# A hybrid attention encoder step: the norm's row factor moved from the activations onto values, queries and keys

## The chip, the cores and the metric

One NeuronCore of a Trainium2 chip runs the whole step in one launch. The metric is the device time in microseconds (us) of that launch; lower is better. Engines are named as in the profile: PE is TensorE (matmuls; PEld are its weight loads), ACT is ScalarE, DVE is VectorE, POOL is GpSimd, and SP is the queue from which all DMA transfers of this kernel are issued.

## The reference

The program is one layer of a streaming encoder on 2048 prompt rows and 32 sample rows of width 1024, all in float32.

```
a = rmsnorm(x, g_attn)                 # x * rsqrt(mean(x*x) + eps) * g, row by row
qa, ka, va, qb, kb, vb = split(a @ w_in)       # 6 x 512 columns
oa = differential attention of qa, ka, va      # 4 heads, two maps each, chunk-causal
ob = band attention of qb, kb, vb              # 8 heads, 64-row chunks and the 8 before
h  = x + concat(norm(oa), norm(ob)) @ w_out
h  = h + relu(norm(h) @ w_up)**2 @ w_down
h  = h + sigmoid(h @ w_ple_gate) * (p @ w_ple_proj)
y  = rmsnorm(h, g_final)
```

Outputs are y and the keys and values of both groups. The sample rows attend to cached keys and values as well. What matters below is the first line: the factor r = rsqrt(mean(x*x) + eps) is one number per row, so (x * r * g) @ W is r times ((x * g) @ W).

## The kernel before, in words

Float32 products are made of three matmuls. Each operand is split into a high part that TensorE takes exactly (`hi`, type fp32r) and the rest (`lo`), and `mm3` (L187) issues hi*hi, hi*lo and lo*hi into one PSUM bank. `split` (L167) makes the parts: a cast on ACT or DVE for `hi`, a subtraction on POOL or DVE for `lo`. `wunit` (L178) loads a 512 KB piece of a weight matrix through one of two staging buffers `wr` and splits it into `wh` and `wl`.

The rows are worked in four blocks of 512 (block 3 has the 32 sample rows too). `prep` (L320) makes the normed activations of a block, 128 rows (a token tile) at a time: load x; ACT squares it and sums each row (L329); `rsqrt` (L195) makes r in three small ACT and four small DVE operations; PE transposes r, broadcast, into `rp` (L334), and ACT copies it to `rb` (L336); PE transposes x in two halves of four 128x128 pieces, each half in one PSUM bank `xp` (L342); ACT copies each half to `xt` (L343), which is stored as xT for the later residual; DVE multiplies each piece by g and rb (L346) into `a32`; DVE casts this to `aH`, POOL subtracts to get `aL`.

`proj` (L359) multiplies by w_in. The values of a group come in two columns of 256; for each column all token tiles of a half are worked (24 matmuls of 256 columns into `vps`), copied from PSUM by ACT (L384), split, and stored. Then for each of four pairs of heads come queries (`kind` 0, scaled by 0.125, L427 and L428) and keys (`kind` 1, L433), 24 matmuls of up to 512 columns each into `qps`. Results go to DRAM scratch, from which the attention loads them.

The order in `run` (L1132): blocks 0 and 1 are normed, then projected for group A (differential); then the first half of group A's attention, the band projections of blocks 0 and 1, woven with `prep` of blocks 2 and 3, band attention, and so on; later attention runs among the MLP's matmuls. In the first stage `prep` uses three PSUM banks of the pool `s`; `prep` of blocks 2 and 3 shares the two banks `mm` with the projections. The order written in the program isn't the order on the engines: a planner with its own estimates of time places every instruction on its engine's queue, from priorities that follow the program's order. Each engine then works its queue strictly in that order. The field `nt` (L139, L1266) is the number of temporary buffers of tag `tmp`, used by `raw_o` (L826) and others.

Of the kernel before, what the change touches and what calls it, by code (L numbers as in the profile page):

```python
# [133 lines left out]
class Kern:  # L134
    def __init__(self, tc, a):
        self.tc = tc
        self.nc = tc.nc
        self.a = a
        self.nt = 4  # L139
# [38 lines left out]
    def wunit(self, src, shape, hi_eng="act", lo_eng="pool"):  # L178
# [3 lines left out]
        hi = self.wp.tile([P] + shape, F32R, tag="wh", bufs=3, name="wh")  # L182
        lo = self.wp.tile([P] + shape, F32R, tag="wl", bufs=3, name="wl")
        self.split(hi, lo, raw, hi_eng, lo_eng)
        return hi, lo
# [9 lines left out]
    def rsqrt(self, pool, src, n, scale, eps, eng, tag="rs", np_=P, bufs=None):  # L195
# [9 lines left out]
        eng.tensor_tensor(y0, y0, v, op=ALU.mult)  # L205
        return y0
# [7 lines left out]
    def consts(self, cp):  # L214
# [13 lines left out]
        self.g_attn = cols("g_attn_s", a["g_attn"][0], 8)  # L228
        self.g_mlp = cols("g_mlp_s", a["g_mlp"][0], 8)
# [90 lines left out]
    def prep(self, b, acts, pp, mm, tag):  # L320
        nc = self.nc
        aH, aL = acts[b]
        for c0, n in toks(b):
# [3 lines left out]
            a32 = pp.tile([P, 8, P], F32, tag="a32", name="a32")  # L327
            st = pp.tile([P, 1], F32, tag="st", name="st")
            nc.scalar.activation(  # L329
                a32[:n].rearrange("p a b -> p (a b)"), x[:n], AF.Square, accum_out=st[:n]  # L330
            )
            r = self.rsqrt(pp, st[:n], 1, 1.0 / D, EPS, nc.vector, "r1", n)
            rp = mm.tile([P, 512], F32, tag=tag, name="rp")
            nc.tensor.transpose(rp[:, :n], r.broadcast_to([n, P]), self.ident[:n, :n])  # L334
            rb = pp.tile([P, P], F32, tag="rb", name="rb")
            nc.scalar.activation(rb[:, :n], rp[:, :n], AF.Copy)  # L336
            xt = pp.tile([P, 8, P], F32, tag="xt", name="xt")
            for h in range(2):
# [4 lines left out]
                nc.scalar.activation(xt[:, 4 * h : 4 * h + 4, :n], xp[:, :, :n], AF.Copy)  # L343
                for k in range(4):
                    kk = 4 * h + k
                    nc.vector.scalar_tensor_tensor(  # L346
                        a32[:, kk, :n], xp[:, k, :n], self.g_attn[:, kk : kk + 1], rb[:, :n],
                        op0=ALU.mult, op1=ALU.mult,
                    )
            self.dma(self.xT[:, :, t0 : t0 + n], xt[:, :, :n])  # L350
            self.split(aH[:, :, c0 : c0 + n], aL[:, :, c0 : c0 + n], a32[:, :, :n], "dve", "pool")
# [6 lines left out]

    def proj(self, half, grp, acts, sg, mm, tp, vs=range(2), gs=range(4)):  # L359
# [3 lines left out]
        nh, dv = (4, 128) if grp == 0 else (8, 64)  # L363
        hc = nh // 2
        vo_p, vo_s = (a["va_p"], a["va_s"]) if grp == 0 else (a["vb_p"], a["vb_s"])
        ko_p, ko_s = (a["ka_p"], a["ka_s"]) if grp == 0 else (a["kb_p"], a["kb_s"])
        for c in vs:
            col = base + 1024 + 256 * c
            wv = W[:, col : col + 256].rearrange("(k p) c -> p k c", p=P)
            u = [self.wunit(wv[:, 4 * i : 4 * i + 4], [4, 256]) for i in range(2)]  # L370
            for b in half:
                aH, aL = acts[b]
                for c0, n in toks(b):
                    t0 = 512 * b + c0
                    ps = mm.tile([P, 512], F32, tag="mm", name="vps")
                    self.mm3(
                        ps[:n, :256],
                        [
                            (aH[:, k, c0 : c0 + n], aL[:, k, c0 : c0 + n], u[k // 4][0][:, k % 4], u[k // 4][1][:, k % 4])
                            for k in range(8)  # L380
                        ],
                    )
                    raw = sg.tile([P, 256], F32, tag="vraw", bufs=2, name="vraw")
                    nc.scalar.activation(raw[:n], ps[:n, :256], AF.Copy)  # L384
                    hl = sg.tile([P, hc, 2, dv], F32R, tag="vhl", bufs=2, name="vhl")
                    r3 = raw.rearrange("p (h d) -> p h d", d=dv)
                    self.split(hl[:n, :, 0], hl[:n, :, 1], r3[:n], "dve", "pool")
                    row = t0 if t0 < SP else t0 + PAST
                    self.dma(
                        self.vS[grp][row : row + n, 512 * c : 512 * c + 512],  # L390
                        hl[:n].rearrange("p a b d -> p (a b d)"),
                    )
                    if t0 >= SP:
                        self.dma(vo_s[0:n, 256 * c : 256 * c + 256], raw[:n])
                    elif grp == 0:
                        self.dma(vo_p[t0 : t0 + n, 256 * c : 256 * c + 256], raw[:n])
                    elif t0 >= SP - 512:
                        self.dma(
                            vo_p[t0 - SP + 512 : t0 - SP + 512 + n, 256 * c : 256 * c + 256], raw[:n]
                        )  # L400
                    yield
# [941 lines left out]
```

## Time and profile before

| | us |
|---|---|
| median of 3 runs (lowest, highest) | 3227.9 (3224.61, 3232.49) |
| profiled execution | 3221.24 |
| its span | 3219.5 |
| PE busy | 3063.0 |
| ACT busy | 1689.7 |
| POOL busy | 1706.1 |
| DVE busy | 1552.4 |

A line of the windows gives the stretch, its length, the busy time and the number of instructions of PE, PEld, DVE, ACT and POOL, the clock granted to PE (1.00 is full), the mean busy share of the DMA engines and GB/s. A line of the groups gives the program line, the engine and operation, output and inputs with shapes, the count, busy us and mean ns, and behind the second bar the idle time before these instructions with what ended it. A line of the waits gives who waited for whom, us in total, how often, and the longest. A line of the order of time gives start and duration. The mean of a matmul (about 290 ns at 256 columns) is its latency; matmuls overlap, so their pace is read from their starts.

### The profile page before, as it was taken

What the parts mean: (1) busy time and instruction counts of PE and PEld (TensorE: products, weight loads), DVE (VectorE), ACT (ScalarE), POOL (GpSimd) and SP (SyncE); (2) the same over time, 40 slices, a digit from 0 to 9 for tenths busy, and PEclk for the clock granted to TensorE, in tenths of its full rate; (3) what the DMA queues carried; (4) which work ended last, traced back from release to release, by engine and by line L of the source; (5) the groups of instructions that cost most, each with busy time, mean ns of one, the idle gap of its engine ahead of it and who ended that gap; (6) DMA issues with size and microseconds to landing.
All of it is one profiled execution on the core that took longest, in us unless ns stands there. A gap on an engine that the chain in (4) does not pass through costs nothing.

```text
span 3219.5 us, 51107 instructions
## 1 busy us (share of the span) xinstructions
PE 3063.0 (95%) x17881; PEld 2687.7 (83%) x17881; DVE 1552.4 (48%) x3952; ACT 1689.7 (52%) x3717; POOL 1706.1 (53%) x2515
## 2 busy tenths in 40 slices
PE   6988989999998999899999999999999999999998
PEld 6877778889887888778788888878789999999988
DVE  5116776444464555576565566636532223223335
ACT  4226776666565766576566666644443322322255
POOL 5446766432345444565554555587954333333387
PEclk9999999999999999999999999999999999999999
DMA  7579876986787653654755444357431111111122
GB/s 235 164 251 264 236 226 205 264 226 182 211 248 215 190 146 105 166 161 137 215 137 143 125 135 124 119 159 252 147 114 47 47 47 47 46 46 47 60 86 88
DMA packets 503272, 487.89 MB, mean 152 GB/s; under 512 B 36924, under 2 KB 392576, under 8 KB 503016
## 3 DMA queue, kind: packets, MB, share of 16 engines
q1 hardware_dynamic: 503016, 484.64, 51.6%
q8 instruction: 141, 2.31, 0.3%
q14 instruction: 115, 0.94, 0.1%
HBM read 378.52 MB, written 109.95 MB: 152 GB/s over the span
## 4 chain that ended last, share of the span: by engine, by line
PE 54%; DMA 4%; DVE 4%; POOL 2%; ACT 2%; issue 1%; SPq 0%; DVEq 0%; POOLq 0%; ACTq 0%
PE ups L192 7%; PE dps L191 7%; PE ups L191 7%; PE ups L193 7%; PE dps L193 7%; PE dps L192 7%; PE s L585 2%; PE gps L191 1%; PE gps L192 1%; PE gps L193 1%; DMA wr<-w_down 1%; PE tpp L657 1%; PE ob L792 1%; POOL wl L165 1%; DVE e L622 1%
## 5 line engine op out<-in xcount | busy, mean ns | idle before, releaser
L165 POOL TENSOR_TENSOR wl<-wr,wh 128x256 fp32r<-128x256 f32 x936 | 694.6, 774 | 479.1 <-ACT wh L170 447.9
L170 ACT ACTIVATE wh<-wr 128x1024 fp32r<-128x1024 f32 x338 | 356.9, 1057 | 573.3 <-PE dps L192 292.6
L1000 DVE TENSOR_TENSOR h<-h,dps 128x512 f32<-128x512 f32 (+1 forms) x640 | 373.2, 585 | 561.5 <-PE dps L193 549.1
L155 POOL TENSOR_TENSOR wl<-wr,wh 128x256 fp32r<-128x256 f32 x416 | 304.9, 764 | 400.9 <-ACT wh L170 384.6
L191 PE MATMUL dps<-uh,wh 128*128 128x512 f32 (+1 forms) x1280 | 457.3, 357 | 7.4 <-DVE h L1000 6.6
L191 PE MATMUL ups<-cH,wh 128*128 128x512 f32 (+1 forms) x1280 | 451.3, 353 | 2.0 <-ACT cH L170 1.0
L192 PE MATMUL ups<-cL,wh 128*128 128x512 f32 (+1 forms) x1280 | 450.7, 352 | 1.9 <-POOL cL L155 1.8
L193 PE MATMUL dps<-uh,wl 128*128 128x512 f32 (+1 forms) x1280 | 450.1, 352 | 0.0
L192 PE MATMUL dps<-ul,wh 128*128 128x512 f32 (+1 forms) x1280 | 449.7, 351 | 0.0
L193 PE MATMUL ups<-cH,wl 128*128 128x512 f32 (+1 forms) x1280 | 449.0, 351 | 0.0
L155 POOL TENSOR_TENSOR ul<-relu,uh 128x136 fp32r<-128x136 f32 (+1 forms) x320 | 199.3, 644 | 158.6 <-ACT uh L170 157.3
L191 PEld LDWEIGHTS dps<-uh,wh 128*128 128x128 f32 x1280 | 241.3, 189 | 41.0 <-DVE h L1000 12.1
L191 PEld LDWEIGHTS ups<-cH,wh 128*128 128x128 f32 x1280 | 240.8, 188 | 34.7 <-ACT relu L965 1.5
L193 PEld LDWEIGHTS dps<-uh,wl 128*128 128x128 f32 x1280 | 240.9, 188 | 32.9
L192 PEld LDWEIGHTS ups<-cL,wh 128*128 128x128 f32 x1280 | 240.9, 188 | 32.3 <-POOL cL L155 2.4
L193 PEld LDWEIGHTS ups<-cH,wl 128*128 128x128 f32 x1280 | 240.8, 188 | 30.0
L192 PEld LDWEIGHTS dps<-ul,wh 128*128 128x128 f32 x1280 | 241.4, 189 | 26.4
L191 PE MATMUL qps<-aH,wh 128*128 128x512 f32 (+1 forms) x640 | 229.2, 358 | 6.1 <-DVE nm L597 2.2
L192 PE MATMUL qps<-aL,wh 128*128 128x512 f32 (+1 forms) x640 | 228.2, 357 | 0.0
L193 PE MATMUL qps<-aH,wl 128*128 128x512 f32 (+1 forms) x640 | 227.5, 355 | 0.0
L585 PE MATMUL s<-ka,q 128*128 128x512 f32 (+3 forms) x768 | 187.4, 344 | 24.4 <-issue 9.2
L591 DVE TENSOR_REDUCE nm<-s 128x1 f32<-128x512 f32 (+3 forms) x256 | 146.9, 587 | 101.6 <-PE s L585 100.5
(230 smaller groups left out, 7084.7 us busy)
## 6 DMA issues: line engine op xcount, KB each, us to landing
wr<-w_up SPq DMA_DIRECT2D x96, 512.0 KB, 4.2
wr<-w_down SPq DMA_DIRECT2D x96, 512.0 KB, 3.8
wr<-w_in SPq DMA_DIRECT2D x74, 512.0 KB, 5.1
q<-qS SPq DMA_DIRECT2D x128, 256.0 KB, 5.5
v<-vSa SPq DMA_DIRECT2D x64, 512.0 KB, 4.0
ka<-kS SPq DMA_DIRECT2D x32, 512.0 KB, 8.0
wr<-w_out SPq DMA_DIRECT2D x32, 512.0 KB, 5.5
wr<-w_ple_gate SPq DMA_DIRECT2D x32, 512.0 KB, 4.3
```

Of the source, the lines that this page charges most:

```text
L155: nc.gpsimd.tensor_tensor(out[:, sl], a[:, sl], b[:, sl], op=op)
L165: nc.gpsimd.tensor_tensor(out[:, sl], a[:, sl], b[:, sl], op=op)
L170: nc.scalar.activation(hi, raw, AF.Copy)
L191: nc.tensor.matmul(ps, lh, rh, start=start and i == 0, stop=False)
L192: nc.tensor.matmul(ps, lh, rl, start=False, stop=False)
L193: nc.tensor.matmul(ps, ll, rh, start=False, stop=stop and i == n - 1)
L585: nc.tensor.matmul(s, q[:, m, hl, P * qi : P * qi + nr], kt[:, m, k0 - kb : k0 - kb + n], start=hl == 0, stop=hl == 1)
L591: nc.vector.tensor_reduce(nmx, s, axis=AX.X, op=ALU.max, negate=True)
L622: nc.vector.scalar_tensor_tensor(e[0][:nr, sl], e[0][:nr, sl], c[:nr, 0, bi : bi + 1], e[1][:nr, sl], op0=ALU.mult, op1=ALU.add)
L657: nc.tensor.transpose(tp[:kn, x, :nr], w[:nr, P * i : P * i + kn], self.ident[:nr, :nr])
L792: nc.tensor.matmul(o[:, qa:qb], vt, pt[:kn, i - kfirst, qa:qb], start=x == 0 and y == 0, stop=x == len(order) - 1 and y == 1,)
L1000: nc.vector.tensor_tensor(hv, hv, ps, op=ALU.add)
```

## The change

The row factor leaves the activations. `prep` now splits x * g straight from the transposed x in PSUM: for each 128x128 piece ACT writes `aH` and DVE writes `aL`, and DVE instead of ACT copies the half to `xt`. The factor r is kept per row in a column tile `rcol` and, transposed, per block in `self.rb`. It is applied later: to values by ACT's copy from PSUM (scale `rcol`), to queries and keys by DVE's multiplication out of PSUM; the high part of queries and keys is now cast by ACT, the low part of both by POOL. A new `vtile` does one token tile of one value column. In the first stage the tiles are normed one after another and each is followed by its two value columns, with all four weight pieces in a pool of their own; `prep` takes PSUM banks of two pools (`s` and `tp`) in turn there. The first x is loaded ahead of the constants, and g_mlp, out_norm_b and subln_g are loaded by a new `gains` later. To make room, `nt` is 3 until the buffers of the MLP open, and the band attention's query tile has two slots instead of three, with a small tile `qn` for the sample's queries.

```diff
@@ __init__
-        self.nt = 4
+        self.nt = 3
@@ wunit: with pool, the pieces go to that pool's 4 buffers
+            hi = pool.tile([P] + shape, F32R, tag="wh0", bufs=4, name="wh0")
+            lo = pool.tile([P] + shape, F32R, tag="wl0", bufs=4, name="wl0")
@@ prep
-        for c0, n in toks(b):
+        for i, (c0, n) in enumerate(toks(b)):
...
-            r = self.rsqrt(pp, st[:n], 1, 1.0 / D, EPS, nc.vector, "r1", n)
-            rp = mm.tile([P, 512], F32, tag=tag, name="rp")
-            nc.tensor.transpose(rp[:, :n], r.broadcast_to([n, P]), self.ident[:n, :n])
-            rb = pp.tile([P, P], F32, tag="rb", name="rb")
-            nc.scalar.activation(rb[:, :n], rp[:, :n], AF.Copy)
...
-                nc.scalar.activation(xt[:, 4 * h : 4 * h + 4, :n], xp[:, :, :n], AF.Copy)
                 for k in range(4):
                     kk = 4 * h + k
+                    g = self.g_attn[:, kk : kk + 1]
+                    hi, lo = aH[:, kk, c0 : c0 + n], aL[:, kk, c0 : c0 + n]
+                    nc.scalar.activation(hi, xp[:, k, :n], AF.Copy, scale=g)
                     nc.vector.scalar_tensor_tensor(
-                        a32[:, kk, :n], xp[:, k, :n], self.g_attn[:, kk : kk + 1], rb[:, :n],
-                        op0=ALU.mult, op1=ALU.mult,
+                        lo, xp[:, k, :n], g, hi.bitcast(F32), op0=ALU.mult, op1=ALU.subtract
                     )
+                nc.vector.tensor_copy(xt[:, 4 * h : 4 * h + 4, :n], xp[:, :, :n])
             self.dma(self.xT[:, :, t0 : t0 + n], xt[:, :, :n])
-            self.split(aH[:, :, c0 : c0 + n], aL[:, :, c0 : c0 + n], a32[:, :, :n], "dve", "pool")
+            r = self.rcol[:n, 4 * b + i : 4 * b + i + 1]
+            self.rsqrt(pp, st[:n], 1, 1.0 / D, EPS, nc.vector, "r1", n, out=r)
+            rp = mm.tile([P, 512], F32, tag=tag, name="rp")
+            nc.tensor.transpose(rp[:, :n], r.broadcast_to([n, P]), self.ident[:n, :n])
+            nc.scalar.activation(self.rb[b][:, c0 : c0 + n], rp[:, :n], AF.Copy)
@@ vtile (the body of the old value loop)
+        nc.scalar.activation(raw[:n], ps[:n, :256], AF.Copy, scale=self.rcol[:n, 4 * b + i : 4 * b + i + 1])
@@ proj, queries and keys
+                        rb = self.rb[b][:, s0 : s0 + n]
                         if kind == 0:
-                            nc.scalar.activation(h_, ps[:, :n], AF.Copy, scale=0.125)
+                            r_ = l_.bitcast(F32)
                             nc.vector.scalar_tensor_tensor(
-                                l_, ps[:, :n], 0.125, h_.bitcast(F32), op0=ALU.mult, op1=ALU.subtract
+                                r_, ps[:, :n], 0.125, rb, op0=ALU.mult, op1=ALU.mult
                             )
                         else:
                             r_ = raw[:, s0 : s0 + n]
-                            nc.scalar.activation(r_, ps[:, :n], AF.Copy)
-                            self.split(h_, l_, r_, "dve", "pool")
+                            nc.vector.tensor_tensor(r_, ps[:, :n], rb, op=ALU.mult)
+                        self.split(h_, l_, r_, "act", "pool")
@@ attn_b
-            q = pool.tile([P, 3, 2, 256], F32R, tag="q", bufs=2, name="q")
-            self.load_q(q[:, :2], gi, (m,), js[0], 2)
+            q = pool.tile([P, 2, 2, 256], F32R, tag="q", bufs=2, name="q")
+            self.load_q(q, gi, (m,), js[0], 2)
@@ run
-            self.consts(cp)
             with ExitStack() as x:
                 pp = opened(x, "pp0", 3, side="right")
+                wv = opened(x, "wv0", 1, side="right")
                 acts = {b: self.actpair() for b in HALVES[0]}
                 for b in HALVES[0]:
-                    drain(self.prep(b, acts, pp, ps_s, "s"))
+                    self.rows(b, sg)
...
+                ring = Rings((ps_s, "s"), (ps_t, "tp"))
+                todo = [(b, i) for b in HALVES[0] for i in range(4)]
+                gen = (y for b in HALVES[0] for y in self.prep(b, acts, pp, ring, "s", first if b == 0 else None))
+                next(gen)
+                units.append(self.vunits(0, 0, pool=wv))
+                next(gen)
+                units.append(self.vunits(0, 1, pool=wv))
+                self.gains(cp)
+                for b, i in todo:
+                    for c in range(2):
+                        self.vtile(b, i, 0, c, units[c], acts, sg, mm)
+                    next(gen, None)
...
-            drain(self.proj(HALVES[0], 0, acts, sg, mm, Rings((ps_t, "tp"))))
+            drain(self.proj(HALVES[0], 0, acts, sg, mm, Rings((ps_t, "tp")), vs=()))
...
+            self.nt = 4
             wk = opened(sq_, "wk", 1)
```

More of the change, by code (lines that the diff above doesn't have):

```diff
@@ L204, in rsqrt @@
         eng.tensor_scalar(v, v, -0.5, 1.5, op0=ALU.mult, op1=ALU.add)
[L205 to L206 removed]
+        out = y0 if out is None else out
+        eng.tensor_tensor(out, y0, v, op=ALU.mult)
+        return out
     def xsrc(self, t0, n):
@@ L362, in proj @@
         base = 1536 * grp
[L363 to L365 removed]
         ko_p, ko_s = (a["ka_p"], a["ka_s"]) if grp == 0 else (a["kb_p"], a["kb_s"])
         for c in vs:
[L368 to L370 removed]
+            u = self.vunits(grp, c)
             for b in half:
[L372 to L400, printed above, removed]
+                for i in range(len(toks(b))):
+                    self.vtile(b, i, grp, c, u, acts, sg, mm)
                     yield
```

76 lines of the change are left out of this document (66 added, 10 removed).

## The prediction

> **What bounds the kernel now.** I read the page first, then windows of 40 us over the first 480 us, then the waits of PE in the two stages that the change touches, then single rows of the order of time.
>
> ```profile
> span 3219.5 us, 51107 instructions
> PE 3063.0 (95%) x17881; PEld 2687.7 (83%) x17881; DVE 1552.4 (48%) x3952; ACT 1689.7 (52%) x3717; POOL 1706.1 (53%) x2515
> ```
>
> ```profile
> 0.00:40.00 40.00, 20.94 (x141) 19.06 (x141) 23.74 (x76) 23.72 (x63) 24.02 (x38) 1.00 0.87 270
> 40.00:80.00 40.00, 34.81 (x260) 33.42 (x261) 18.04 (x53) 10.60 (x26) 22.79 (x32) 0.92 0.64 202
> 80.00:120.00 40.00, 40.00 (x206) 33.67 (x206) 4.81 (x10) 9.29 (x15) 17.98 (x25) 1.00 0.56 184
> ...
> 240.00:280.00 40.00, 37.81 (x206) 32.19 (x205) 18.49 (x70) 22.05 (x60) 21.93 (x32) 1.00 0.95 269
> 280.00:320.00 40.00, 33.52 (x245) 31.64 (x243) 34.39 (x131) 31.16 (x106) 32.38 (x48) 0.91 0.91 260
> 320.00:360.00 40.00, 35.82 (x204) 29.74 (x205) 33.48 (x114) 29.71 (x90) 31.51 (x45) 1.00 0.87 245
> 360.00:400.00 40.00, 40.00 (x220) 34.42 (x219) 26.18 (x72) 26.93 (x69) 29.50 (x43) 1.00 0.78 218
> 400.00:440.00 40.00, 34.74 (x272) 32.81 (x270) 32.67 (x109) 31.69 (x95) 26.61 (x37) 1.00 0.79 234
> 440.00:480.00 40.00, 31.51 (x184) 27.36 (x184) 28.92 (x80) 25.48 (x72) 25.97 (x36) 0.91 0.79 221
> ```
>
> TensorE is the bound: 3063.0 of 3219.5 us, so only 156.5 us of its time is idle, and the change neither adds nor removes a matmul or a transpose. It can gain only idle time of PE. In the first two windows (columns: length, busy PE, PEld, DVE, ACT, POOL, clock, DMA share, GB/s) that is 19.1 + 5.2 = 24.3 us. From 80 us PE is full, so what is saved ahead of 80 us moves all that follows. From 240 to 480, where the first attention blocks run between projections and the norms of blocks 2 and 3, it is 2.2 + 6.5 + 4.2 + 0 + 5.3 + 8.5 = 26.7 us, with DVE and ACT both near 75 to 85% in the worst windows. The change touches these two stages most.
>
> ```profile
> PE rp L334 <- DVE rsy L205: 11.7, 3, 10.4
> PE vps L191 <- DVE rsv L203: 4.4, 2, 2.8
> PE vps L191 <- ACT vraw L384: 2.7, 3, 1.6
> ```
>
> These waits (us in total, times, longest) are of the first 130 us. 10.4 us is PE's first instruction: nothing can be transposed until the square, the root and the reciprocal of the first tile are done. The next one is a matmul that stands behind DVE's root arithmetic.
>
> ```profile
> 3.03 1.38 SPq L146 DMA_DIRECT2D x<-x_prompt  x3
> 6.78 1.06 ACT L329 ACTIVATE a<-x 128x1024 f32<-128x1024 f32 x1 [4.76 <-DMA x<-x_prompt]
> 10.68 1.91 PE L342 MATMUL xp<-ident,x 128*128 128x128 f32 x8
> 17.22 0.58 PE L191 MATMUL vps<-wh,aH 128*128 128x256 f32 x1
> 18.40 6.10 POOL L165 TENSOR_TENSOR aL<-a,aH 128x256 fp32r<-128x256 f32 x8
> ...
> 86.60 0.40 PE L191 MATMUL qps<-aH,wh 128*128 128x512 f32 x1
> ```
>
> In order of time: x is issued at 3.03 behind four small loads and lands by 6.78; transposes at 10.68, the first value matmul at 17.22, the low half aL on POOL only from 18.40. All sixteen value tiles are through when the first query matmul starts at 86.60. That is the mark of this stage.
>
> **The change part by part.** *Start.* The x load is issued first, so it lands after the same 3.75 us (6.78 - 3.03) from 0.74 us on: about 4.5. Transposes no longer wait for the root: 4.5 against 10.7, about -6. The two halves of the weights follow x and the gain on SP; three small loads now stand behind the second x. At some 0.46 us per issue (1.38 for three) that frees the weights by about 2 us; their cast (1.06 us on ACT, 3 us of lows on POOL) ends about 9 to 13. The first value matmul comes at about 8 instead of 17.2.
>
> *New startup waits.* Both value columns are now worked per tile, so the second column's weights are needed within two tiles. They come through the same two staging buffers: the third load waits until POOL has read the first.
>
> ```profile
> wr<-w_in SPq DMA_DIRECT2D x5, 512.0 KB, 5.8
> L165 POOL TENSOR_TENSOR wl<-wr,wh 128x256 fp32r<-128x256 f32 x24 | 17.8, 776 | 11.8 <-ACT rsy L201 11.0 <-ACT wh L170 0.8
> L384 ACT ACTIVATE vraw<-vps 128x256 f32<-128x256 f32 x16 | 6.0, 382 | 24.5 <-PE vps L193 6.9 <-DMA va_p<-vraw 6.9 <-POOL vhl L165 4.5
> L336 ACT ACTIVATE rb<-rp 128x128 f32<-128x128 f32 x8 | 2.2, 274 | 7.1 <-PE rp L334 7.1
> L346 DVE SCALAR_TENSOR_TENSOR a<-xp,g_attn_s,rb 128x128 f32<-128x128 f32 x64 | 17.6, 341 | 5.4 <-ACT rsy L200 3.0 <-ACT xt L343 2.4
> ```
>
> So: issue at 10 (7 + 4 x 0.776), 5.8 to land, 1 to cast: 17; PE, in its fixed order, idles about 2 to 4 us there. From then on PE sets the pace. Its work is known from a dense stretch:
>
> ```profile
> 203.02 0.29 PE L192 MATMUL vps<-wl,aH 128*128 128x256 f32 x1
> ...
> 204.20 0.29 PE L193 MATMUL vps<-wh,aL 128*128 128x256 f32 x1
> ```
>
> Ten steps in 1.18 us, 0.118 each: 384 value matmuls are 45.3 us; 72 transposes at 0.12 to 0.24 (1.91 / 8 above) are 9 to 17. Per token tile that is 48 x 0.118 + 9 x 0.18 = 7.3 us. Beside it ACT has 1.06 + 0.6 of root + 8 copies at 0.274 + rb 0.27 + 2 values at 0.38 = 4.9, DVE 8 x 0.341 + 2 copies at 0.69 (as the query row L428 below, also 512 out of PSUM) + root and casts of about 2 = 6. Both fit, DVE narrowly. POOL loses its 4 x 0.76 per tile. On SP the 32 stores of values now stand among the x loads and xT stores; at 0.46 us they take 15 of some 65 us, and no wait of PE hangs on them but the buffers of the next value tile. DMA moves what it moved before, in less time; its share of 0.87 in the first window leaves some room only. By this sum: 8 us of start, 45.3 + 13 of work, 2 to 4 for the second column, and 4 of the old 9 us of small waits and cold clock (0.92 in the second window) left: about 73 to 75 instead of 86.6. I take -12; -5 if DMA holds it at 0.95 share all along, -17 with no late weights.
>
> *Queries and keys.* Old: ACT copies from PSUM, then DVE (queries) or DVE and POOL in SBUF (keys). New: DVE alone multiplies by the row factor out of PSUM, ACT casts, POOL subtracts.
>
> ```profile
> L165 POOL TENSOR_TENSOR aL<-a,aH 128x256 fp32r<-128x256 f32 x65 | 48.6, 778 | 23.4 <-DVE aH L172 9.8 <-DVE nm L597 6.5 <-DMA x<-x_prompt 2.7
> L155 POOL TENSOR_TENSOR ql<-kr,qh 128x256 fp32r<-128x256 f32 x48 | 35.1, 751 | 33.2 <-DVE qh L172 18.1 <-issue 11.8 <-DMA pS<-ppl 3.3
> L155 POOL TENSOR_TENSOR ql<-kr,qh 128x136 fp32r<-128x136 f32 x32 | 15.6, 508 | 14.2 <-DVE qh L172 7.5 <-issue 5.7 <-DVE stb L759 0.9
> L428 DVE SCALAR_TENSOR_TENSOR ql<-qps,qh 128x512 fp32r<-128x512 f32 x24 | 16.5, 689 | 53.8 <-ACT qh L427 51.4 <-DMA qS<-ql 2.4
> L172 DVE CAST qh<-kr 128x512 fp32r<-128x512 f32 x24 | 14.4, 602 | 48.7 <-ACT kr L433 46.0 <-issue 1.8 <-POOL sqacc L155 0.7
> L433 ACT ACTIVATE kr<-qps 128x512 f32<-128x512 f32 x24 | 14.1, 587 | 21.7 <-PE qps L193 21.7
> ```
>
> POOL gains for the queries what it has for the keys (35.1 + 15.6 = 50.7) and loses aL (48.6): level. DVE pays 0.69 for 0.60 per key block, ACT about the same. Each such block has 24 matmuls in front of it, at least 4.7 us of PE (40.0 / 206 in the window from 80), so nothing is late on PE; the PSUM bank is free after one DVE operation instead of ACT and DVE. 0, between -2 and +2.
>
> *The split of x times g from PSUM.* ACT makes aH of a 128x128 slice, DVE aL from the same slice. In the changed kernel's own order of waits every aH but the first of a bank waits for DVE, and every aL for ACT. The two engines take turns on one bank, eight handoffs instead of two. Now a bank goes like this:
>
> ```profile
> 305.90 1.06 PE L342 MATMUL xp<-ident,x 128*128 128x128 f32 x4
> 307.00 0.60 ACT L343 ACTIVATE xt<-xp 128x512 f32<-128x512 f32 x1 [0.54 <-PE xp L342]
> 307.99 1.12 DVE L346 SCALAR_TENSOR_TENSOR a<-xp,g_attn_s,rb 128x128 f32<-128x128 f32 x4
> ```
>
> ACT 0.60, DVE 1.12, done at 309.11: 3.2 us after the transposes began, 2.1 after they ended. New: 4 x (0.274 + 0.28) + a copy of 0.69 on DVE = 2.9 us of bare work, and with 0.4 us behind other work at each handoff (307.00 + 0.60 to 307.99) about 6. In the first stage five banks of two pools take turns, so it is hidden. In blocks 2 and 3 the transposes use the two banks of the projections, and a bank held 3 us longer can starve the matmuls that fill PE.
>
> ```profile
> PE vps L191 <- DVE a L346: 1.4, 2, 1.0
> ```
>
> Of the 26.7 idle us only this 1.4 is a wait of PE for such a bank (130 to 480 us). If the wait grows with the time that the bank is held, from 3.2 to about 6, it is 1.3 more; I take +2. The bounds: -6 (aL off POOL and no root ahead of the transposes shorten the norm) and, with 3 us fully exposed for half of the 16 banks, +24.
>
> The Trainium skill, "PSUM — Partial Sum Buffer", section "PSUM bank collisions raise a hardware error", says that ScalarE and VectorE may not read one bank at the same time, so a scheduler has to order even two reads. The trace agrees in that DVE's L346 is seen waiting for ACT's xt (2.4 us in the row of the first 90 us). By this rule the split costs the turns; without it ACT and DVE would overlap and the item would be 0.
>
> *The rest.* Query tiles of the band attention shrink, and its last queries get a buffer of their own: 0, same loads. Three instead of four temporaries until the MLP's buffers open: the eight loads of the output activations go through three slots; hidden by MLP and output matmuls that PE has there, at most +3. The planner puts band attention some 30 to 50 us of PE work earlier against the projections from the middle of the projections on; the last third has the same PE order as before. PE stays as densely filled: 0, +-6.
>
> Sum: -12 + 0 + 2 + 0 = -10 against the profiled 3221.24 us (3219.5 span and 1.7 around it). That run lies 6.7 under the median of 3227.9, so I forecast 3227.9 - 10 = about 3218 for the median.
>
> **The rivals.** *A, the taking of turns costs more than the start wins (slower).* Where: 240 to 480 us, banks of the projections. For it: ACT and DVE run at 75 to 85% there, so each handoff queues. Against: the 1.4 us above. At the full +24, -12 + 24 = +12: 3240. It decides from +12, which is 0.75 us of PE per bank over 16 banks.
>
> *B, the start does not speed up much.* DMA is the bound of the first 40 us (0.87) and the second column's weights are late; first query matmul at 82: -5 + 2 = -3: 3225.
>
> *C, the middle gains too.* With the low half off POOL and the roots off the way, a third of the 26.7 us goes: -12 - 9 = -21: 3207.
>
> **How the numbers follow.** The forecast 0.45, A 0.15, B 0.2, C 0.2. A measurement of this kernel tells about 0.3%, 9.7 us, from no change. The forecast sits on that line with a little more than half of it beyond: faster 0.27 + 0.2 from C = 0.47; same 0.18 + 0.17 of B + 0.04 of A = 0.39; slower 0.11 from A and 0.03 from B = 0.14. Range: from C, 3204, to most of A, 3236.
>
> **What the profile after would show.** First transposes at about 4.5 us and first query matmul at 73 to 75 (82: B). PE busy in the first 40 us near 28 instead of 20.9. A dip of PE near 14 to 18 us on the lows of the second column. The idle of 240 to 480, moved 12 us earlier, near 28; if over 36, with waits of projection matmuls for aL, it is A; if under 20, C. POOL's total near 1706. I would be wrong above all if the reordered middle, which I put at 0, gains or loses more than 6.

## The result and the profile after

The changed kernel takes 3237.97 us (median of 6 runs, 3231.36 to 3247.09) against 3228.24 us before (6 runs, 3224.61 to 3232.49). The ratio on record is 1.0044, 95% interval 1.0029 to 1.0058: slower by 0.44% (the two medians alone give 0.30%). The forecast was 3218 us, with a range from 3204 to 3236.

The head of the page after, of an execution of 3245.35 us:

```profile
span 3243.3 us, 51236 instructions
...
PE 3089.2 (95%) x17881; PEld 2708.8 (84%) x17881; DVE 1550.1 (48%) x3969; ACT 1722.1 (53%) x3819; POOL 1700.4 (52%) x2530
```

TensorE does the same 17881 matmuls and idles as long as before (154.1 us, before 156.5), but is *busy* 26.2 us longer. That points to the granted clock. In the trace's record of the clock, the stretches at half speed, without the one at the end, add up to 92.2 us before and 146.8 after. Half of the extra 54.6 us is 27.3, about the whole difference. All of them but the last are multiples of 3.413 us long. The Trainium skill, "TensorE: Matmul & The Clock Gate", section "What's actually happening", says that the clock falls to half after an idle window of about 3.4 us; the trace's lengths agree with it. The profiled execution is an unlucky one: its mean clock is 0.976, that of the other five runs 0.979 to 0.981. So the two profiled executions lie 24.1 us apart and the medians 9.7.

Windows of the kernel after (columns as before the prediction: length, busy PE, PEld, DVE, ACT, POOL, granted clock, DMA share, GB/s):

```profile
0.00:40.00 40.00, 26.24 (x169) 24.31 (x170) 23.11 (x76) 29.36 (x87) 20.59 (x35) 0.96 0.91 278
40.00:80.00 40.00, 40.00 (x321) 38.63 (x320) 20.21 (x65) 19.31 (x57) 11.83 (x18) 1.00 0.75 245
230.00:480.00 250.00, 218.49 (x1305) 192.54 (x1306) 174.20 (x599) 182.73 (x555) 146.01 (x215) 0.92 0.79 223
480.00:640.00 160.00, 143.18 (x886) 125.06 (x885) 82.23 (x302) 102.38 (x270) 79.06 (x129) 0.94 0.75 220
230.00:640.00 410.00, 361.67 (x2190) 317.60 (x2191) 256.43 (x900) 285.11 (x825) 225.07 (x343) 0.93 0.78 222
```

The same three later windows of the kernel before:

```profile
230.00:480.00 250.00, 222.56 (x1363) 195.41 (x1361) 176.06 (x578) 170.13 (x494) 173.61 (x246) 0.97 0.85 242
480.00:640.00 160.00, 153.34 (x1088) 142.19 (x1089) 88.09 (x299) 104.62 (x276) 87.60 (x140) 1.00 0.83 234
230.00:640.00 410.00, 375.91 (x2451) 337.60 (x2450) 264.15 (x876) 274.75 (x768) 261.21 (x385) 0.98 0.84 239
```

The start came nearly as forecast: the first 80 us hold 66.2 us of PE instead of 55.8. The middle went the other way. Although all work reaches it some 14 us earlier, PE starts 261 fewer matmuls and transposes between 230 and 640 us (2190, before 2451), at a lower clock. Which ones are missing is seen from the last query or key matmul and the first of the output projection. Rows of the two tiles (line, engine, operation, tile, count: ns min/median/max, first and last start), after:

```profile
L197 PE MATMUL qps<-aH,wl x640: 282/390/628, 73.1 to 937.5; 128*128 128x512 f32 x96, 128*128 128x272 f32 x64
L195 PE MATMUL ops<-oact,wh x256: 282/389/628, 944.7 to 2286.5; 128*128 128x512 f32 x64, 128*128 128x272 f32 x64
```

and before:

```profile
L193 PE MATMUL qps<-aH,wl x640: 283/390/628, 87.1 to 897.5; 128*128 128x512 f32 x96, 128*128 128x272 f32 x64
L191 PE MATMUL ops<-oact,wh x256: 283/388/632, 905.8 to 2268.1; 128*128 128x512 f32 x64, 128*128 128x272 f32 x64
```

The projections begin 14.0 us earlier and end 40.0 us later. They are what fills PE while attention waits for ScalarE and VectorE. Their accumulators share two PSUM banks with the transposes of the norms of blocks 2 and 3. One such bank after, in order of time:

```profile
263.13 0.60 PE L357 MATMUL xp<-ident,x 128*128 128x128 f32 x4
...
264.26 0.35 ACT L362 ACTIVATE aH<-xp,g_attn_s 128x128 fp32r<-128x128 f32 x1
...
264.73 0.34 DVE L363 SCALAR_TENSOR_TENSOR aL<-xp,g_attn_s,aH 128x128 fp32r<-128x128 f32 x1
...
265.32 0.35 ACT L362 ACTIVATE aH<-xp,g_attn_s 128x128 fp32r<-128x128 f32 x1
...
266.12 0.34 DVE L363 SCALAR_TENSOR_TENSOR aL<-xp,g_attn_s,aH 128x128 fp32r<-128x128 f32 x1
...
266.50 0.37 ACT L362 ACTIVATE aH<-xp,g_attn_s 128x128 fp32r<-128x128 f32 x1
...
267.88 0.34 DVE L363 SCALAR_TENSOR_TENSOR aL<-xp,g_attn_s,aH 128x128 fp32r<-128x128 f32 x1
...
268.73 0.35 ACT L362 ACTIVATE aH<-xp,g_attn_s 128x128 fp32r<-128x128 f32 x1
...
270.49 0.34 DVE L363 SCALAR_TENSOR_TENSOR aL<-xp,g_attn_s,aH 128x128 fp32r<-128x128 f32 x1
270.75 0.68 DVE L366 COPY xt<-xp 128x512 f32<-128x512 f32 x1
```

From 263.13 to 271.43 it is held for 8.3 us, against 3.2 in the prediction's example of before. (The high half at 267.37 and the low half at 269.69, left out here, are of the second bank, which is filled from 266.59 on: that high half waits for PE, as only the first of a bank does.) Taken over all 18 banks of the two blocks in this way (first transpose to end of the last read), the median hold is 9.6 us after and 4.4 before.

What PE waited for after, 230 to 640 us (total, times, longest), the longest waits:

```profile
PE s L612 <- DMA ka<-kS: 8.8, 4, 3.6
PE s L612 <- ACT e L626: 8.6, 9, 2.1
PE sb L782 <- DMA q<-qS: 5.0, 2, 2.7
PE rp L371 <- DVE xt L366: 4.2, 3, 2.4
```

Only the last row, 4.2 us, is plainly a wait for a bank that the split holds. The others are attention matmuls that stand alone. PE works in a fixed order, and in the changed kernel's order fewer projections stand between them (the column "early" below).

### The profile page after: what moved, and what is told of

Read it like the earlier page. It is cut to its first block, busy times and chain, and to the rows that moved or that the text cites. A ratio compares the mean times of both kernels' runs of the same rounds, so it can differ in the third digit from the quotient of the medians.

```text
span 3243.3 us, 51236 instructions
## 1 busy us (share of the span) xinstructions
PE 3089.2 (95%) x17881; PEld 2708.8 (84%) x17881; DVE 1550.1 (48%) x3969; ACT 1722.1 (53%) x3819; POOL 1700.4 (52%) x2530
## 4 chain that ended last, share of the span: by engine, by line
PE 73%; DMA 12%; DVE 7%; ACT 4%; issue 2%; SPq 1%; POOL 1%; DVEq 0%; POOLq 0%; ACTq 0%
PE dps L195 7%; PE dps L196 7%; PE ups L195 7%; PE dps L197 7%; PE ups L196 6%; PE ups L197 6%; PE qps L195 3%; PE qps L196 3%; PE qps L197 3%; PE s L612 3%; PE ob L822 2%; DMA oraw<-oT 2%; PE gps L197 2%; PE gps L195 2%; PE gps L196 2%
## 5 line engine op out<-in xcount | busy, mean ns | idle before, releaser
L626 ACT ACTIVATE e<-s,nm 128x512 f32<-128x512 f32 (+3 forms) x256 | 155.1, 611 | 79.1 <-DVE nm L618 68.2
```

Source lines behind the costliest of these rows:

```text
L626: nc.scalar.activation(dst, src, AF.Exp, bias=nmx, accum_out=z[:nr, m, bi : bi + 1])
```

## Experiments

Each kernel ran in several rounds beside the kernel before, whose medians there were 3222.5 to 3227.0; so compare kernels by the ratios. To see where time goes, I lined up every trace with that of before by matmul work done (each matmul weighted by the pace of its width) and read how far it is behind (+) or ahead (-) at four points, named by the time of the kernel before: 190 us (end of the start), 738 us (end of the middle), 912 us (the projections have run out, the output projection has begun), 3206 us (the end). "Hold" is the median hold of the 18 banks (for e11, of block 2 and of block 3). "Middle" is the second less the first, "gap" the time from the last query or key matmul to the first of the output projection. "Early" is the PE time of the projection matmuls that stand before the first band score in PE's order, at 0.46 ns a column (0.118 us for 256); the order is fixed, so this figure does not change from run to run. The others are worked out from the one profiled execution of each kernel, which can differ from the median by some us, and the middle also depends on the weights: other plausible ones move it by up to some 8 us (in e5; the changed kernel's stays between +42 and +47). So only large differences in it are read below.

| kernel | median us | ratio (95%) | hold | at 190 | at 738 | at 912 | at 3206 | middle | gap | early |
|---|---|---|---|---|---|---|---|---|---|---|
| before | 3228.2 | 1 | 4.4 | 0 | 0 | 0 | 0 | 0 | 8.2 | 376 |
| after | 3238.0 | 1.0044 (1.0029 to 1.0058) | 9.6 | -14.1 | +32.7 | +18.6 | +23.8 | +46.8 | 7.2 | 344 |
| e1 start alone | 3225.5 | 0.9999 (0.9988 to 1.0009) | 3.8 | -2.0 | +0.4 | +5.8 | +4.7 | +2.4 | 31.9 | 390 |
| e2 split as before | 3206.1 | 0.9939 (0.9924 to 0.9954) | 3.9 | -13.9 | -25.1 | -19.5 | -18.4 | -11.2 | 33.8 | 394 |
| e3 old start | 3255.9 | 1.0090 (1.0073 to 1.0108) | 10.2 | -2.4 | +42.8 | +28.9 | +44.6 | +45.2 | 8.5 | 350 |
| e4 grouped halves | 3235.0 | 1.0031 (1.0019 to 1.0043) | 5.4 | -9.1 | +14.7 | +20.0 | +22.0 | +23.8 | 32.9 | 394 |
| e5 copy, then split | 3213.0 | 0.9968 (0.9956 to 0.9980) | 3.0 | -14.3 | -24.0 | -3.4 | -4.6 | -9.7 | 44.1 | 406 |
| e6 VectorE both halves | 3217.7 | 0.9983 (0.9969 to 0.9998) | 6.9 | -13.4 | +12.3 | +5.7 | -2.4 | +25.7 | 7.6 | 374 |
| e7 split as before, all blocks | 3222.0 | 1.0002 (0.9991 to 1.0013) | 4.1 | +3.7 | -5.5 | -0.7 | +3.3 | -9.2 | 32.2 | 394 |
| e8 weave 2 | 3197.9 | 0.9922 (0.9907 to 0.9937) | 4.4 | -14.9 | -12.6 | -16.7 | -19.3 | +2.3 | 7.6 | 377 |
| e9 last low from the bank | 3223.7 | 0.9993 (0.9979 to 1.0006) | 5.8 | -16.3 | -5.7 | -0.4 | +0.6 | +10.6 | 32.2 | 394 |
| e10 after, weave 2 | 3254.1 | 1.0076 (1.0060 to 1.0091) | 9.8 | -14.0 | +46.7 | +32.9 | +32.7 | +60.7 | 7.6 | 344 |
| e11 block 3 as before | 3218.5 | 0.9967 (0.9952 to 0.9982) | 9.7, 3.6 | -15.7 | -6.6 | -13.5 | -8.3 | +9.1 | 5.6 | 359 |
| e12 bank read once | 3215.7 | 0.9971 (0.9961 to 0.9982) | 2.4 | -16.1 | -18.4 | -11.8 | -12.4 | -2.3 | 33.9 | 394 |

### The parts, undone one at a time: e1 to e4

Three theories stood at first, named in the texts below: T1 (the split's turns in blocks 2 and 3), T2 (the row factor on queries and keys) and T3 (chance of the order). e1 is the kernel before with the new start of `run` alone (its pool `pp0` has two buffers of each tag, for room):

```diff
@@ run, kernel before
-                for b in HALVES[0]:
-                    drain(self.prep(b, acts, pp, ps_s, "s"))
+                ring = Rings((ps_s, "s"), (ps_t, "tp"))
+                gen = (y for b in HALVES[0] for y in self.prep(b, acts, pp, ring, "s", first if b == 0 else None))
...
+                for b, i in todo:
+                    for c in range(2):
+                        self.vtile(b, i, 0, c, units[c], acts, sg, mm)
+                    next(gen, None)
```

> The kernel before with only the new start (x and the first values tile by tile); the row factor, the old norm with x times g times r, and the old queries and keys stay. Theory T1 (the start wins some 14 us; the turns of ScalarE and VectorE on the x banks in the norms of blocks 2 and 3, and the order of TensorE's work that they bring about, lose some 25 to 40): 3210 to 3218 us, first query matmul near 75 us, no band scores before some 570 us of the span. T2 (the loss comes from the row factor on the queries and keys): the same here, 3210 to 3218. T3 (any shift in the timing of the start scrambles the middle, and the clock dips that follow cost what the start wins): 3228 to 3240.

e2 is the changed kernel with the old making of x times g in blocks 2 and 3:

```diff
@@ prep, per bank of x
+                if b >= 2:
+                    nc.scalar.activation(xt[:, 4 * h : 4 * h + 4, :n], xp[:, :, :n], AF.Copy)
+                    for k in range(4):
+                        nc.vector.tensor_scalar(a32[:, kk, :n], xp[:, k, :n], g, None, op0=ALU.mult)
+                    continue
...
+            if b >= 2:
+                self.split(aH[:, :, c0 : c0 + n], aL[:, :, c0 : c0 + n], a32[:, :, :n], "dve", "pool")
```

> The changed kernel, but blocks 2 and 3 make x times g as the kernel before did: ScalarE copies the bank, VectorE multiplies the bank into SBUF, the cast on VectorE and the low half on GpSimd read SBUF. The row factor on values, queries and keys and the new start stay. T1: 3210 to 3220 us, half-clock stretches of the span back near 92 us in all (147 in the changed kernel). T2 (queries and keys): 3235 to 3240, as the changed kernel. T3: anything between 3225 and 3245.

e3 is the changed kernel with the old start:

```diff
@@ run, changed kernel
-                ring = Rings((ps_s, "s"), (ps_t, "tp"))
...
+                for b in HALVES[0]:
+                    drain(self.prep(b, acts, pp, ps_s, "s"))
...
-            drain(self.proj(HALVES[0], 0, acts, sg, mm, Rings((ps_t, "tp")), vs=()))
+            drain(self.proj(HALVES[0], 0, acts, sg, mm, Rings((ps_t, "tp"))))
```

> The changed kernel with the start of the kernel before: the norms of blocks 0 and 1 run out first, then the value columns one after the other. The row factor and the split from PSUM stay. Its order of TensorE's work in the middle is that of the changed kernel. T1: the loss stays and the start's 14 us go too: 3248 to 3256 us. T3 (the new start is what upsets the middle): 3225 to 3232, as the kernel before.

e4 keeps every instruction of the changed kernel and orders those of a bank otherwise, in all blocks:

```diff
@@ prep, per bank of x
                 for k in range(4):
                     nc.scalar.activation(aH[:, kk, ...], xp[:, k, :n], AF.Copy, scale=g)
+                for k in range(4):
                     nc.vector.scalar_tensor_tensor(aL[:, kk, ...], xp[:, k, :n], g, aH[:, kk, ...], ...)
```

> The changed kernel with the same instructions, only written in another order for each bank of x: first ScalarE's four high halves, then VectorE's four low halves, then the copy (two changes of engine on a bank instead of eight). TensorE's order in the middle comes out as in the kernel before. T1: most of the loss goes: 3212 to 3224 us. If the loss is the work on the bank itself (as many reads from PSUM, whatever their order): 3235 to 3240. T2: 3235 to 3240.

e2 settles where the loss is: 3206.1 us, 1.05% of the kernel before (34 us) below the changed kernel, with the new queries and keys, row factor, buffers and start all in place. Its row of the windows:

```profile
230.00:640.00 410.00, 381.69 (x2505) 346.09 (x2504) 272.73 (x868) 280.35 (x769) 285.39 (x427) 0.96 0.82 238
```

2505 matmuls and transposes instead of 2190. T2, the queries and keys, is out. e3 agrees, within T1's range: without the new start the loss stays, and 0.46% (15 us) comes on top. That is what the start is worth. But e1, the new start alone, is worth nothing (0.9999), between T1's 3210 to 3218 and T3's 3228 to 3240: its first query matmul starts at 84.7 us, not 75.

e4 missed: 3235.0 is the low end of what was expected if the reads themselves cost, whatever their order. The turns fell from eight to two and the hold from 9.6 to 5.4, yet only 0.13% came back, part of it eaten by the start (the same grouping in blocks 0 and 1 leaves it 5 us slower). The middle still loses 23.8 us of the 46.8, though TensorE's order there is close to e2's (394 us early in both). Here waits for the banks are seen; from its list of waits, 230 to 640 us:

```profile
PE xp L357 <- ACT vraw L404: 4.7, 4, 2.7
PE xp L357 <- DVE xt L369: 3.6, 2, 1.8
```

So "turns" was too narrow a name. Two new theories: P, what counts is how long the bank is held; Q, it is the work and handoffs in the queues of ScalarE and VectorE.

### Bank or queues: e5, e6 and e9

e5 makes the halves from a copy, with the changed kernel's count of instructions and its alternation:

```diff
@@ prep, blocks 2 and 3
+                    nc.vector.tensor_copy(xt[:, 4 * h : 4 * h + 4, :n], xp[:, :, :n])
                 for k in range(4):
+                    s = xt[:, kk, :n] if b >= 2 else xp[:, k, :n]
-                    nc.scalar.activation(hi, xp[:, k, :n], AF.Copy, scale=g)
+                    nc.scalar.activation(hi, s, AF.Copy, scale=g)
-                    nc.vector.scalar_tensor_tensor(lo, xp[:, k, :n], g, ...)
+                    nc.vector.scalar_tensor_tensor(lo, s, g, ...)
-                nc.vector.tensor_copy(xt[:, 4 * h : 4 * h + 4, :n], xp[:, :, :n])
```

> The changed kernel, but in blocks 2 and 3 VectorE copies each bank of x to SBUF first, and ScalarE's high and VectorE's low halves are made from that copy, tile by tile: the same count of instructions and of handoffs between the two engines as in the changed kernel, but the bank is free after one copy. Theory P (the loss is the bank of the projections' PSUM pool, held some 9.6 us instead of 4.3): 3203 to 3214 us, as the run with the split as before (3206). Theory Q (the loss is in the queues of ScalarE and VectorE, which beside attention A are three quarters busy: 4 high halves of 0.37 us a bank instead of one copy of 0.6, and handoffs that hold the softmax up): 3228 to 3240, as the run with the halves grouped (3235).

e6 takes the alternation away instead, and leaves both halves to one engine:

```diff
@@ prep, blocks 2 and 3
+                    nc.scalar.activation(xt[:, 4 * h : 4 * h + 4, :n], xp[:, :, :n], AF.Copy)
-                    nc.scalar.activation(hi, xp[:, k, :n], AF.Copy, scale=g)
+                    nc.vector.tensor_scalar(hi, xp[:, k, :n], g, None, op0=ALU.mult)
                     nc.vector.scalar_tensor_tensor(lo, xp[:, k, :n], g, ...)
```

> The changed kernel, but in blocks 2 and 3 ScalarE only copies each bank (as in the kernel before), and VectorE alone makes both halves from PSUM: no handoff within a bank, 13 us less of ScalarE's work and some 14 us more of VectorE's over the 18 banks, nothing for GpSimd. Q, if ScalarE's queue and the handoffs are the cause: 3206 to 3218. P: the bank is held for 8 operations of 0.34 us on one engine, some 4 to 6 us: 3206 to 3218 too. If what counts is that the low halves leave GpSimd and come onto VectorE or ScalarE, whichever of them: 3228 to 3240.

e9 is e5 with one operand changed, so that the last low half holds the bank:

```diff
@@ prep of e5
-                        lo, s, g, hi.bitcast(F32), op0=ALU.mult, op1=ALU.subtract
+                        lo, xp[:, k, :n] if k == 3 else s, g, hi.bitcast(F32), op0=ALU.mult, op1=ALU.subtract
```

> The copy-then-split run (3213) with one operand changed: the last of the four low halves of a bank is made from the bank, not from the copy, so that the bank is held until the split is done, with the same instructions and handoffs. Theory P (the hold of one of the two banks that the projections use): the middle loses again, the time goes to 3225 to 3240, and the median hold from 3.0 us to over 5. Theory Q (the work in ScalarE's and VectorE's queues): no change, 3207 to 3219.

e5's 3213.0 us is within P's range and far from Q's: with as many handoffs and as much work for ScalarE and VectorE, but a bank free after 3.0 us, the middle no longer loses (-9.7 us). A bank of e5 in order of time, over in 1.3 us:

```profile
264.04 0.60 PE L357 MATMUL xp<-ident,x 128*128 128x128 f32 x4
...
264.68 0.69 DVE L359 COPY xt<-xp 128x512 f32<-128x512 f32 x1
```

and its window:

```profile
230.00:640.00 410.00, 375.43 (x2496) 342.37 (x2497) 271.33 (x841) 281.04 (x793) 260.64 (x393) 0.97 0.80 233
```

e9's window, with the same instructions:

```profile
230.00:640.00 410.00, 369.76 (x2350) 333.19 (x2349) 256.32 (x827) 273.09 (x773) 252.74 (x381) 0.94 0.77 222
```

With the one operand the hold goes from 3.0 to 5.8 us, 146 instructions leave the window and the middle loses 20.3 us. The order went with it: 394 us of projections stand ahead of band attention, not 406. The time rises by 0.25% to 3223.7, just below P's 3225 and outside Q's 3207 to 3219. e6 has no turns and little for ScalarE to do, and its total (3217.7) is at the upper end of what both theories expected. By that total the third case, that taking the low halves off GpSimd is what costs, is out. But its bank is held for 6.9 us and its middle loses 25.7 us, as much as the grouped e4. Its order is that of the kernel before (374 and 376 us early), so here the loss came with the longer hold and without a new order; some of it comes back behind the middle (+12.3 at 738, -2.4 at the end). The Trainium skill, "PSUM — Partial Sum Buffer", section "PSUM bank collisions raise a hardware error", says that no two engines may be on one bank and quadrant at once, reads included. The turns of the changed kernel (264.26, 264.73, 265.32 above) agree with that, and in none of the fourteen traces do ACT and DVE read such a bank at the same moment: the program orders them, and what a collision would do is not shown. But e6, with one engine for both halves, shows that a bank is held for 6.9 of the 9.6 us without any turns.

### How the start is made: e7

e7 is e2 with the old split in all four blocks (its conditions `b >= 2` become true for every block).

> The run with the split as before, with it in blocks 0 and 1 too, which leaves the split from PSUM nowhere; the row factor on values, queries and keys, and the new start, stay. If the start's 14 us come from the split from PSUM: 3214 to 3222 us, first query matmul at 80 to 85. If they come from taking the row factor's chain out of the way of the first halves: 3204 to 3210, first query matmul at 73 to 76.

3222.0 us, 0.63% above e2: the first case, at the end of its range, and the first query matmul comes even later than expected there, at 90.4. So the same split from PSUM that loses in blocks 2 and 3 earns the whole start in blocks 0 and 1, where no projection shares its banks and PE waits for its result. The new start alone (e1), with the row factor moved (e7), or with the split but the old order (e3) has 2.0, none (it loses 3.7) and 2.4 of the 14 us at 190 us; only all three together have it.

### Order: e8 and e10

e8 is e2, e10 the changed kernel, each with one number changed:

```diff
-            weave(self.proj((1,), 1, acts, sg, mm, tp), lifted(self.prep(2, acts, pp, mm, "mm")), 3)
+            weave(self.proj((1,), 1, acts, sg, mm, tp), lifted(self.prep(2, acts, pp, mm, "mm")), 2)
```

> The run with the split as before, with block 2's norm woven in after every second step of the projections instead of every third: a shift that changes no work. Theory T3 (any shift of the order in the middle costs or gains 20 to 30 us by where the clock dips fall): away from 3206 by more than 12 us. P and Q: 3200 to 3214.

> The changed kernel with block 2's norm woven in after every second step instead of every third, the shift that took 5 us off the run with the split as before. T3 (the loss is a chance of the order and its clock dips): away from 3238 by more than 12 us. P: 3230 to 3246, since each bank is held as long as before.

e8 is the fastest of all: 3197.9 us, 2 us below the range of P, and 0.78% below the kernel before. e10 is 0.3% slower than the changed kernel: 16 us, more than P allowed and what T3 had forecast, where e8's 8 us were less than T3's 12. In the middle the closer weave costs about the same 14 us in both (-11.2 to +2.3, and +46.8 to +60.7). So a change of order without one of the split moves the middle by some 14 us; the split, with the order that it brings, moved it by 46.8. T3 as the cause of the whole loss is out, as a scatter of this size it stays.

### A part of the blocks, and less than one read: e11 and e12

e11 is the changed kernel with the old split in block 3 alone (the conditions of e2 with `b >= 3`).

> The changed kernel with the old split in block 3 alone; block 2 keeps the split from PSUM. P, with the loss of some 33 us (3238 less 3206) shared by the two blocks by their banks, 8 in block 2 and 10 in block 3: 3215 to 3228. If one of the blocks carries it all: 3203 to 3210, or 3235 to 3241.

3218.5 us, within P's range: 0.77% below the changed kernel, 0.28% above e2. Block 3 carries most of the loss, more than its 10 of 18 banks; what is left for block 2 is little beyond the noise.

e12 is e8 with VectorE reading ScalarE's copy:

```diff
-                            a32[:, kk, :n], xp[:, k, :n], self.g_attn[:, kk : kk + 1], None, op0=ALU.mult
+                            a32[:, kk, :n], xt[:, kk, :n], self.g_attn[:, kk : kk + 1], None, op0=ALU.mult
```

> The weave-2 run (3198) with one operand changed: in blocks 2 and 3 VectorE multiplies ScalarE's copy of the bank, not the bank itself, so that the bank is read once and free after one copy; the instructions and the work of each engine are the same. P, by what the other runs lost between their holds (some 7 us per us of median hold above 3): the hold falls from 4.4 to between 1.5 and 3 us and the time by 5 to 12 us, to 3186 to 3194. If the hold no longer matters below some 4.5 us: 3194 to 3202. If the later multiply holds the halves up: 3202 to 3212.

A miss: 3215.7 us, 0.5% above e8 and beyond the range of every theory. The hold did fall, to 2.4 us, and the middle gained 4.6 us. What was won there is lost afterwards. (The two profiled executions are only 6.9 us apart, so the larger part of the 0.5%, 16 us, is not in these traces.) The gap column says where: e8's projections last until the output projection can begin, e12's and e5's have run out before. From e8, the two tiles and a window:

```profile
L197 PE MATMUL qps<-aH,wl x640: 282/390/632, 72.2 to 882.1; 128*128 128x512 f32 x96, 128*128 128x272 f32 x64
L195 PE MATMUL ops<-oact,wh x256: 283/389/775, 889.7 to 2244.9; 128*128 128x512 f32 x64, 128*128 128x272 f32 x64
850.00:900.00 50.00, 45.59 (x287) 41.59 (x287) 32.37 (x93) 35.95 (x74) 22.13 (x36) 0.93 0.90 266
```

and from e5:

```profile
L197 PE MATMUL qps<-aH,wl x640: 282/391/628, 73.0 to 853.5; 128*128 128x512 f32 x96, 128*128 128x272 f32 x64
L195 PE MATMUL ops<-oact,wh x256: 282/389/497, 897.6 to 2264.1; 128*128 128x512 f32 x64, 128*128 128x272 f32 x64
850.00:900.00 50.00, 39.22 (x200) 33.34 (x200) 29.93 (x103) 35.54 (x75) 9.44 (x18) 0.76 0.83 233
```

In e5's 44.1 us without projections PE has band attention alone: 200 instructions in these 50 us instead of 287, at a clock of 0.76. Over the whole table, the seven kernels with a gap of some 32 us or more lose 4.8 to 20.6 us between 738 and 912, and the six others, before aside, gain 4.1 to 14.1. The order decides which kernels these are: the seven have 390 to 406 us of projections ahead of band attention, all others 344 to 377. So e12 runs out because its order, unlike e8's, does more of them early (394 instead of 377). That is a reading of thirteen traces; no run was made to change the gap alone.

## Why the prediction was wrong

The step that failed is "The split of x times g from PSUM", which took +2 with bounds of -6 and +24. Measured, undoing it in blocks 2 and 3 is worth 34 us (e2), and lined up by work the middle loses 46.8. Three parts of its working were wrong, and a term was missing.

- *The size of the hold.* "About 6 instead of 3.2" was 9.6 instead of 4.4 in the median. The two figures were not of one kind: 3.2 runs from the first transpose, and 6 is only the work behind the transposes, so their 1.1 us (305.90 to 306.96 in the prediction's rows) were left out. I took 0.274 and 0.28 us for the halves; they take 0.35 to 0.37 and 0.34. And I counted 0.4 us behind other work at each handoff; the low halves of the bank shown above start 0.1, 0.45, 1.0 and 1.4 us behind the end of their high halves (the last: 268.73 + 0.35 to 270.49).
- *The price of the hold.* I scaled the one wait that the list of before showed, 1.4 us. In this kernel, whose order is fixed beforehand, little of such a cost appears as a wait for the bank: the changed kernel's list has some 4 us of it. It appears as projections that stand later in PE's order, 261 fewer instructions by 640 us, and as attention waiting alone. By the table the middle shows no loss that follows the hold up to about 4.4 us, and loses some 9 us per us beyond it: +46.8 for 5.2 (e4 more, 23.8 for 1.0, which this leaves open). That is near half of the added hold, 18 banks x 5.2 us = 94 us of one bank of two; the bound of +24 had the same half, of 3 us and 16 banks.
- *The turns as the cause.* They are one way to a long hold. e6 has none and loses half as much.
- *What the loss is made of.* "It can gain only idle time of PE" left the clock out of the sum. The idle time stayed as it was (154.1 us, before 156.5); PE's busy time grew by 26.2 us between the two profiled executions, which the stretches at half speed account for (27.3).

"The rest", put at 0 +-6 for band attention drawn 30 to 50 us earlier, was not independent. The figure was right: 344 us of projections stand ahead of band attention instead of 376, 32 us fewer. But that belongs to the split by turns: with it the figure is 344 to 350 also with another start or weave (e3, e10), and where it is undone (e2) it is 394. How much of the 46.8 is the order and how much is waiting within it, no run separates. A long hold needs no new order to lose (e6, 25.7 with the order of before; e4, 23.8 with that of e2), and order alone (e8, e10) moves 14.

The other steps held in the main. The start, -12 with bounds -5 and -17, measured -14 at the first query matmul: from the order of time after,

```profile
4.47 1.94 PE L357 MATMUL xp<-ident,x 128*128 128x128 f32 x8 [4.47 <-DMA x<-x_prompt]
8.67 0.58 PE L195 MATMUL vps<-wh,aH 128*128 128x256 f32 x1 [2.26 <-ACT wh L170]
```

4.5 and about 8 were forecast; the first query matmul came at 72.7 instead of 73 to 75 (the terms of that sum add up to 72.3 to 74.3). PE was busy for 26.2 of the first 40 us, forecast near 28. Its dip came at 16 to 20 us (1.73 of 4 us busy), forecast for 14 to 18, but not on the low halves: it waited 1.5 us for the row factor `rcol` and 0.8 for ACT's cast of the second column. A second dip, PE idle for 3.6 us up to 31.86, was not forecast at all: ACT, in its fixed order, stood 2.9 us at the cast of a weight that had not landed, with the copy of the values `vraw` behind it. Rival B is out. What I had not seen is that this gain needs the split from PSUM (e7). Queries and keys, 0: e2 contains them and is 0.61% faster than before, so they take nothing that shows there. The smaller buffers and `nt` are in e2 as well; neither was run alone.

Rival A had the right place and, at 3240, nearly the time, at a chance of 0.15. That nearness is luck in part: the middle lost 46.8 us and not 24, and 14.1 of them came back between 738 and 912. Its sign did not come: I looked for an idle of over 36 us between 240 and 480, with projections waiting for the low half. It was 30.9 (26.6 before). The loss also lies from 480 to 640, where the idle went from 6.7 to 16.8 us, and in the clock: 0.93 instead of 0.98 over the 410 us. Rival C's sign, an idle under 20 us there, came in none of the fourteen kernels; but where the bank is free early the idle falls to 22.4 (e2) and 22.0 us (e5) and the middle does not lose.

## What to carry to other kernels

Before moving work onto a PSUM bank, count how long the bank is held, first write to last read with queueing (the same way before and after), and who else uses that pool; price it as a share of those banks taken away, not by the waits that the old profile shows. The same rewrite can gain where the banks are spare and PE waits for its result, and lose where they feed the filler: apply it by place. Taking a mix of both here (the split from PSUM in the first two blocks, the copy and old split in the others, a closer weave) gives 3197.9 us, 0.78% below the kernel before.

## What was not expected of the hardware

With equal idle time the same matmuls took 26.2 us more of busy time: it is where the idle pieces fall that decides. Each stretch at half clock is at least 3.4 us long, and there were 26 of them instead of 15, the last one aside. The falls lie on a grid of 3.413 us, and PE need not be idle all through a window of it: in the window ahead of a fall it was busy for less than half in 35 of the 41 falls of the two traces (0.66 at most), and of their 1763 windows at full speed that no fall followed only one was below half. By that, two idle pieces of 1 us in one window can bring a stretch at half speed that the same pieces in two windows would not. A copy of four pieces in one ScalarE operation takes 0.60 us, four scaled operations 4 x 0.35 to 0.38, so the split by pieces is 0.8 to 0.9 us longer per bank on ScalarE, besides the handoffs. From one start to the next that follows closely it is 0.25 us against 0.48, so of ScalarE's time it takes some 0.5 us more.
